# Half of each down projection by Strassen's scheme, in a float32 encoder block on one core

## The chip, the core and the metric

The kernel runs on one core of a Trainium2 chip. TensorE (PE in the profile; its weight loads are PEld) multiplies, VectorE (DVE) and ScalarE (ACT) work element by element, GpSimd (POOL) does next to nothing here, and SyncE (SP) issues the DMAs. The metric is the device time of one execution in microseconds. Less is better.

## The reference

One layer on x of 256 positions by 2048 channels, all in float32. Only the last part matters here:

```python
u = _rmsnorm(h, norm_mlp_g[layer])
a = jnp.einsum('bsd,df->bsf', u, w_up[layer])
a = jnp.square(jax.nn.relu(a))
h = h + jnp.einsum('bsf,fd->bsd', a, w_down[layer])
...
return _rmsnorm(h, norm_final_g)
```

w_up is 2048 x 8192, w_down 8192 x 2048. Before it come an input projection, a Fourier branch, eight heads of attention and an output projection; the change leaves their code alone.

## The kernel before

**Numbers.** A float32 operand is written as a high part, rounded for the fast matmul, and a low part, the rest. `split` (line 128) casts the high part on ScalarE and subtracts on VectorE. A product is three matmuls, high by high, high by low, low by high: `mm3` (line 138).

**Weights.** `_order` (line 39) lists the chunks of all weights, each a tile of 128 x 2048 (1 MB), in the order in which the program uses them. `load_next` (line 151) loads a chunk into `w_raw` and splits it into `w_hi` and `w_lo` in two halves of 1024 columns. `chunk` (line 179) hands out the next one and calls `load_next` so that AHEAD = 2 further chunks are under way. The pool has AHEAD + 1 = 3 buffers of each name, so a chunk is cast into the buffers of the chunk three earlier, once TensorE is through with that one.

**The MLP.** The 8192 hidden channels go in NGRP = 4 groups of 2048. In each group:

- 16 columns of the up projection (`column`, line 229): 16 matmuls of 128x512 with the high weights, then 16 of 128x256 with the low ones. `total` (line 260) adds the two halves of the result, `up` (line 558) applies relu, the norm's factor and the square, and splits the result into row j of `y_hi` and `y_lo`.
- 4 strips of the down projection (`strip`, line 204): each makes 512 output channels from four chunks, 24 matmuls of 128x512 per chunk (2 blocks of 128 positions by 4 rows by 3). The result is added to h (`gh` in the profile).

In the last group the fourth strip is the tail (from line 591). Its chunks are multiplied by `products`: the first 128 positions in one PSUM tile of 512 columns, the others in two of 256. The finished strips before it are squared, summed and multiplied by the final norm's weights on the way, and `ending` does the last norm and stores.

**Order.** Each engine runs its instructions in the order in which a scheduler has put them when the program is built. It may put later work ahead of an instruction that it expects to wait. The chunk loads keep the order of `_order` on SP's queue. PSUM has two pools of four tiles: `acc` for columns and strips, `aux` for the rest.

Of the kernel before, what the change touches and what calls it, by code (L numbers as in the profile page):

```python
# [29 lines left out]
CK = KT // NN  # L30
NGRP = DFF // D
AHEAD = 2
FIRST = (4, 4, 2, 2, 2)
WARM = 9
FEW = 224
MIDDLE = 11


def _order():

    todo = []

    def rows(name, row0, col0):
        todo.extend((name, row0 + c * CK * P, CK, col0, NS) for c in range(NN))

    def cols(name, col0):
        todo.append((name, 0, KT, col0, P))  # L50

    rows("w_in", 0, 0)
    rows("w_in", 0, NS)
    for a in range(2):
        rows("w_in", 0, 3 * FOURIER + a * NS)
        for hd in range(a * 4, a * 4 + 4):
            cols("w_in", FOURIER + hd * HD)
            cols("w_in", 2 * FOURIER + hd * HD)
    for n in range(NN):
        rows("w_out", 0, n * NS)  # L60
    for gi in range(NGRP):
        for j in range(KT):
            cols("w_up", gi * D + j * P)
        for n in range(NN):
            rows("w_down", gi * D, n * NS)
    return todo


# [1 line left out]
def tile_block(ctx: ExitStack, tc: tile.TileContext, gx_t, x, w_all, w_f, g_fin,  # L70
# [6 lines left out]
    ps_acc = ctx.enter_context(tc.tile_pool(name="ps_acc", bufs=4, space=bass.MemoryType.PSUM))  # L77
    ps_aux = ctx.enter_context(tc.tile_pool(name="ps_aux", bufs=4, space=bass.MemoryType.PSUM))

    def acc():  # L80
        return ps_acc.tile([P, NS], F32, name="acc")

    def aux():
        return ps_aux.tile([P, NS], F32, name="aux")
# [66 lines left out]
    def load_next():  # L151
        i = len(loaded)
        raw = wpool.tile([P, D], F32, name="w_raw")
        hi = wpool.tile([P, D], F32R, name="w_hi")
        lo = wpool.tile([P, D], F32R, name="w_lo")
        cuts = FIRST[i] if i < len(FIRST) else 1
# [12 lines left out]
        loaded.append((hi.rearrange("p (k n) -> p k n", k=nk), lo.rearrange("p (k n) -> p k n", k=nk)))  # L169

    def load_x(k0, nk):
        cols = slice(NG + k0 * S if k0 else 0, NG + (k0 + nk) * S)
# [53 lines left out]
                part()  # L226
        return ps

    def column(r, parts=None, need=None):

        ps = acc()
        hi, lo = chunk()

        def large(kt):
            nc.tensor.matmul(ps, hi[:, kt, :], r[:, kt, :], start=kt == 0, stop=False)  # L237

        def few_columns(kt):
            nc.tensor.matmul(ps[:, S:], lo[:, kt, :], r[:, kt, :S], start=False, stop=kt == KT - 1)  # L240
# [42 lines left out]
    def across(inv, room):  # L283

        ps = aux()[:, :S]
        for m in range(NM):
            b = room()
            nc.vector.tensor_scalar_mul(out=b, in0=ones, scalar1=inv[:, m:m + 1])
            nc.tensor.transpose(ps[:, m * P:(m + 1) * P], b, ident)
        return ps  # L290
# [257 lines left out]
    att_ctx.close()  # L548

    mlp = ctx.enter_context(tc.tile_pool(name="mlp", bufs=1))  # L550
    junk = mlp.tile([P, NS], F32, name="junk")
# [6 lines left out]
    def up(ps, hidden, j):  # L558
        r = mlp.tile([P, S], F32, name="relu", bufs=2)
        nc.vector.scalar_tensor_tensor(out=r, in0=total(ps, mlp), scalar=0.0, in1=inv_u, op0=ALU.max, op1=ALU.mult)  # L560
        q = mlp.tile([P, S], F32, name="sq", bufs=2)
        nc.scalar.activation(q, r, AF.Square)  # L562
        split(hidden[0][:, j, :], hidden[1][:, j, :], q)

    ss3 = small(NM * NN, NN)
    for gi in range(NGRP):
        pool = acts if gi % 2 else mlp
        hidden = [pool.tile([P, KT, S], F32R, name=f"y_{s}") for s in ("hi", "lo")]
        for j in range(KT):
            if gi == 0 and j == 0:  # L570
                ps = column(u2, parts=(4, 6, 8), need=KT - CK)
                inv2 = inverse(sums(ss2, "n2"), "n2")
                nc.vector.tensor_copy(out=inv_u, in_=across(inv2, lambda: mlp.tile([P, S], F32, name="relu", bufs=2)[:, :P]))
            else:
                ps = column(u2)
            up(ps, hidden, j)
        for n in range(NN):
            final = gi == NGRP - 1
            if final and n == NN - 1:
                break  # L580
            ps = strip(*hidden)
            ns = slice(n * NS, (n + 1) * NS)
            for m in range(NM):
                hs = h[m][:, ns]
                nc.vector.tensor_add(out=hs, in0=hs, in1=ps[m])  # L585
                if final:
                    squares(ss3, m, n)
                    nc.vector.tensor_mul(out=hs, in0=hs, in1=g_b[:, ns])


    NH2 = NS // 2
    tail = [[(acc(), slice(0, NS))], [(aux()[:, :NH2], slice(0, NH2)), (aux()[:, :NH2], slice(NH2, NS))]]
    base = small(NM)
    got = []

# [79 lines left out]
def _tiles(weights):  # L675

    todo = _order()
    out = np.empty((len(todo), P, D), np.float32)
    for i, (name, row0, nk, col0, n) in enumerate(todo):
        block = weights[name][row0:row0 + nk * P, col0:col0 + n]  # L680
        out[i] = block.reshape(nk, P, n).transpose(1, 0, 2).reshape(P, D)
    return out
# [27 lines left out]
```

## Time and profile before

| what | us |
|---|---|
| median of 3 runs | 1023.94 (1023.74 to 1024.06) |
| the profiled execution's own time | 1024.08 |
| its span, first to last instruction | 1022.3 |
| TensorE busy with matmuls | 1012.7 |
| VectorE busy | 610.7 |
| ScalarE busy | 496.3 |

The profile is of one execution. A row of a stretch (a window) gives its length, then for PE, PEld, DVE, ACT and POOL the busy us and, as (x..), the instructions, then the granted clock of TensorE (1.00 is full), the DMA engines' share and GB/s. A row of the timeline gives start, duration, engine, line, operation, output <- input, shape and count, and in brackets the idle time of the engine before it with what ended it. The busy time of matmuls is modelled, and they are pipelined: their spacing says more than their duration.

### The profile page before, as it was taken

What the parts mean: (1) busy time and instruction counts of PE and PEld (TensorE: products, weight loads), DVE (VectorE), ACT (ScalarE), POOL (GpSimd) and SP (SyncE); (2) the same over time, 40 slices, a digit from 0 to 9 for tenths busy, and PEclk for the clock granted to TensorE, in tenths of its full rate; (3) what the DMA queues carried; (4) which work ended last, traced back from release to release, by engine and by line L of the source; (5) the groups of instructions that cost most, each with busy time, mean ns of one, the idle gap of its engine ahead of it and who ended that gap; (6) DMA issues with size and microseconds to landing.
All of it is one profiled execution on the core that took longest, in us unless ns stands there. A gap on an engine that the chain in (4) does not pass through costs nothing.

```text
span 1022.3 us, 13002 instructions
## 1 busy us (share of the span) xinstructions
PE 1012.7 (99%) x5254; PEld 869.2 (85%) x5254; DVE 610.7 (60%) x846; ACT 496.3 (49%) x741; POOL 1.3 (0%) x10
## 2 busy tenths in 40 slices
PE   9999999999999999999999999999999999999997
PEld 7888888888888888888888888888888888888886
DVE  7975775775456665545656545556655446565553
ACT  7754645554446454333555433354543334554441
POOL 0000000000000000000000000000000000000000
PEclk9999999999999999999999999999999999999999
DMA  9663745444565554555555555555545555545532
GB/s 328 229 226 117 267 168 201 164 166 165 188 224 191 180 205 168 203 196 181 200 201 174 202 180 191 206 192 179 206 169 202 199 180 198 199 176 201 182 147 83
DMA packets 32683, 195.10 MB, mean 191 GB/s; under 512 B 3568, under 2 KB 6128, under 8 KB 10608
## 3 DMA queue, kind: packets, MB, share of 16 engines
q1 hardware_dynamic: 32624, 194.28, 53.7%
q8 instruction: 41, 0.67, 0.3%
q14 instruction: 18, 0.15, 0.0%
HBM read 192.17 MB, written 2.10 MB: 190 GB/s over the span
## 4 chain that ended last, share of the span: by engine, by line
PE 97%; DMA 1%; SPq 0%; DVE 0%; ACT 0%; issue 0%; ACTq 0%
PE acc L237 29%; PE acc L140 16%; PE acc L141 16%; PE acc L139 16%; PE acc L240 15%; PE aux L139 1%; PE aux L141 1%; PE aux L140 1%; DMA w_raw<-w_all 1%; SPq L93 0%; PE aux L538 0%; PE aux L493 0%; DVE w_lo L132 0%; ACT w_hi L131 0%; ACT gh L633 0%
## 5 line engine op out<-in xcount | busy, mean ns | idle before, releaser
L132 DVE TENSOR_TENSOR w_lo<-w_raw,w_hi 128x1024 fp32r<-128x1024 f32 (+1 forms) x356 | 424.0, 1209 | 281.0 <-ACT w_hi L131 204.0
L131 ACT CAST w_hi<-w_raw 128x1024 fp32r<-128x1024 f32 (+1 forms) x356 | 354.1, 1038 | 251.5 <-PE acc L141 228.2
L237 PE MATMUL acc<-u,w_hi 128*128 128x512 f32 x1280 | 309.5, 391 | 0.0
L237 PEld LDWEIGHTS acc<-u,w_hi 128*128 128x128 f32 x1280 | 234.8, 188 | 45.1
L139 PE MATMUL acc<-w_hi,y_hi 128*128 128x512 f32 x624 | 243.7, 391 | 0.0
L141 PE MATMUL acc<-w_hi,y_lo 128*128 128x512 f32 x624 | 242.9, 389 | 0.0
L140 PE MATMUL acc<-w_lo,y_hi 128*128 128x512 f32 x624 | 242.9, 389 | 0.0
L240 PEld LDWEIGHTS acc<-u,w_lo 128*128 128x128 f32 x1280 | 165.1, 191 | 6.2
L240 PE MATMUL acc<-u,w_lo 128*128 128x256 f32 x1280 | 168.4, 283 | 0.0
L141 PEld LDWEIGHTS acc<-w_hi,y_lo 128*128 128x128 f32 x624 | 117.2, 188 | 24.6
L140 PEld LDWEIGHTS acc<-w_lo,y_hi 128*128 128x128 f32 x624 | 117.2, 188 | 23.8
L139 PEld LDWEIGHTS acc<-w_hi,y_hi 128*128 128x128 f32 x624 | 117.2, 188 | 23.7
L562 ACT ACTIVATE sq<-relu 128x256 f32<-128x256 f32 x64 | 26.7, 418 | 160.7 <-DVE relu L560 160.7
L132 DVE TENSOR_TENSOR y_lo<-sq,y_hi 128x256 fp32r<-128x256 f32 x64 | 27.3, 426 | 58.8 <-ACT y_hi L131 58.8
L140 PE MATMUL acc<-w_lo,u 128*128 128x512 f32 x120 | 47.1, 392 | 0.5 <-DVE w_lo L132 0.5
L141 PE MATMUL acc<-w_hi,u 128*128 128x512 f32 x120 | 46.8, 390 | 0.0
L139 PE MATMUL acc<-w_hi,u 128*128 128x512 f32 x120 | 46.4, 393 | 0.3 <-ACT w_hi L131 0.3
L263 DVE TENSOR_TENSOR total<-acc,total 128x256 f32<-128x256 f32 x80 | 33.5, 418 | 2.7 <-ACT total L262 2.7
L262 ACT COPY total<-acc 128x256 f32<-128x256 f32 x80 | 29.2, 365 | 8.0 <-PE acc L240 8.0
L585 DVE TENSOR_TENSOR gh<-gh,acc 128x512 f32<-128x512 f32 x30 | 20.5, 684 | 16.8 <-PE acc L141 16.8
L140 PEld LDWEIGHTS acc<-w_lo,u 128*128 128x128 f32 x120 | 22.6, 188 | 5.2 <-DVE w_lo L132 1.1
L131 ACT CAST y_hi<-sq 128x256 fp32r<-128x256 f32 x64 | 26.0, 406 | 2.0
(141 smaller groups left out, 473.5 us busy)
## 6 DMA issues: line engine op xcount, KB each, us to landing
w_raw<-w_all SPq DMA_DIRECT2D x171, 1024.0 KB, 4.8
w_raw<-w_all SPq DMA_DIRECT2D x6, 512.0 KB, 7.9
w_raw<-w_all SPq DMA_DIRECT2D x8, 256.0 KB, 4.5
gh<-x SPq DMA_DIRECT2D x8, 256.0 KB, 7.1
out<-gh SPq DMA_DIRECT2D x6, 256.0 KB, 2.4
gh<-gx_t SPq DMA_DIRECT2D x4, 256.0 KB, 6.6
wf<-w_f SPq DMA_DIRECT2D x4, 256.0 KB, 4.9
g_b<-g_fin SPq DMA_DIRECT2D x1, 1024.0 KB, 4.3
```

The source lines that it names most:

```text
L131: nc.scalar.copy(out=hi, in_=src)
L132: nc.vector.tensor_tensor(out=lo, in0=src, in1=f32(hi), op=ALU.subtract)
L139: nc.tensor.matmul(ps, l_hi, r_hi, start=first, stop=False)
L140: nc.tensor.matmul(ps, l_hi, r_lo, start=False, stop=False)
L141: nc.tensor.matmul(ps, l_lo, r_hi, start=False, stop=last)
L237: nc.tensor.matmul(ps, hi[:, kt, :], r[:, kt, :], start=kt == 0, stop=False)
L240: nc.tensor.matmul(ps[:, S:], lo[:, kt, :], r[:, kt, :S], start=False, stop=kt == KT - 1)
L262: nc.scalar.copy(out=t, in_=ps[1])
L263: nc.vector.tensor_tensor(out=t, in0=ps[0], in1=t, op=ALU.add)
L562: nc.scalar.activation(q, r, AF.Square)
L585: nc.vector.tensor_add(out=hs, in0=hs, in1=ps[m])
```

## The change

In each group half of the down projection's work, output channels 0 to 1023, is done by Strassen's scheme in Winograd's form. The hidden activations are taken as 2 x 2 blocks: positions 0 to 127 and 128 to 255, hidden rows 0 to 7 and 8 to 15. The weights are also 2 x 2 blocks: the same rows by output channels 0 to 511 and 512 to 1023. The eight block products become seven. For this each of four blocks of activations and of four blocks of weights is a sum or difference of original ones, formed before the split into high and low parts. Output channels 1024 to 2047 are done as before ("plain").

- **`_mlp`** lists a group's steps. The columns now go in pairs, j and j + 8, and four of the eight *seven steps* lie between them; the other four lie between the chunks of the two plain strips. Step s takes one chunk that holds rows s and s + 8 of the weights for 1024 output channels, and makes six of the seven products, three matmuls each: 18 of 128x512 into six PSUM tiles, held from step 0 to step 7. The seventh product goes in two chunks of its own ("apart"), 12 matmuls each. In the last group the seven steps are packed closer towards the end, and the apart chunks go between them.
- **`quadrants`** prepares a seven step's chunk. VectorE makes four subtractions of 512 columns in place in `w_raw`, between these ScalarE casts two blocks into `b_hi`, and VectorE subtracts for `b_lo`; then `w_hi` and `w_lo` get the inner and the outer halves. So a chunk has three casts and seven VectorE instructions for two and two. `b_hi` and `b_lo` have one buffer each.
- **`sums_of`** makes the four sums of activations for a pair of columns: four VectorE instructions of 128 columns in place in `sq`, then a split of 512 columns into `s_hi` and `s_lo` (five buffers).
- **The sums of products.** In each group four of the products are added to `kept` (copied in the first), two straight into h, and the apart product into h. After the last group nine additions put `kept` into the four output blocks, and `weigh` squares and multiplies these. All of this lies in program order ahead of the tail's first chunk.
- **PSUM.** `acc` becomes two names of two tiles. The columns, plain strips and the apart product take `first`; two of the six products take `second`, four take `aux`. All groups now write the one `y_hi`, `y_lo`.

The core of the diff (the host's `_tiles` lays the 1 MB chunk out to match):

```diff
+    for j in range(HALF):
+        todo.extend((("up", j, 0), ("up", j + HALF, 0)))
+        if j in (2, 4, 6):
+            seven(j // 2 - 1)
+    seven(3)
...
+        p_hi = mlp.tile([P, 2, NS], F32R, name="b_hi")
+        p_lo = mlp.tile([P, 2, NS], F32R, name="b_lo")
...
+        nc.scalar.copy(out=p_hi, in_=pure)
+        less(b12, b12, b11)
+        less(p_lo, pure, f32(p_hi))
+        less(b22, b22, b12)
+        nc.scalar.copy(out=hi[:, inner], in_=raw[:, inner])
+        less(b11, b22, b11)
+        less(b21, b22, b21)
+        nc.scalar.copy(out=outer(hi), in_=outer(raw))
+        less(lo[:, inner], raw[:, inner], f32(hi[:, inner]))
+        less(outer(lo), outer(raw), f32(outer(hi)))
...
+                for ps, l, r in ((p1, tile_of(i, 0), b11), (p3, s4, b22), (p5, s1, t1), (p7, s3, t3),
+                                 (p6, s2, t2), (p4, tile_of(i + HALF, 1), t4)):
+                    mm3(ps, *l, *r, i == 0, i == HALF - 1)
+                if i == HALF - 1:
+                    for k, ps in ((k1, p1), (k5, p5), (k7, p7), (k6, p6)):
+                        if gi:
+                            add(k, ps)
+                        else:
+                            nc.scalar.copy(out=k, in_=ps)
+                    add(c12, p3)
+                    add(c21, p4, ALU.subtract)
...
+    add(c11, k1)
+    add(k6, k1)
+    for block, ks in ((c12, (k6, k5)), (c21, (k6, k7)), (c22, (k6, k5, k7))):
+        for k in ks:
+            add(block, k)
+    for m in range(NM):
+        for n in range(2):
+            weigh(m, n)
```

How it moves instructions is shown at three places. In these rows a number behind a name tells buffers apart, w_lo<-w_raw is the low half of a chunk's split, and line 189 is `split`, 244 a subtraction of `quadrants`, 353 and 650 a column's total and relu, 662 to 665 `sums_of`.

VectorE in the columns of the last group, before: one column after the other, five instructions each.

```order
L132 TENSOR_TENSOR w_lo_7386<-w_raw_7384,w_hi_7385 128x1024
L263 TENSOR_TENSOR total_7375<-acc_7333,total_7375 128x256
L132 TENSOR_TENSOR w_lo_7386<-w_raw_7384,w_hi_7385 128x1024
L560 SCALAR_TENSOR_TENSOR relu_7374<-total_7375,inv_k_2752 128x256
L132 TENSOR_TENSOR y_lo_6782<-sq_7379,y_hi_6781 128x256
```

The same engine and place now, around the chunk of seven step 2 (w_raw_7846):

```order
L244 TENSOR_TENSOR w_raw_7846<-w_raw_7846 128x512
L189 TENSOR_TENSOR w_lo_7791<-w_raw_7789,w_hi_7790 128x1024 x2
L353 TENSOR_TENSOR total_7781<-acc_7738,total_7781 128x256
L244 TENSOR_TENSOR b_lo_7851<-w_raw_7846,b_hi_7850 128x1024
L650 SCALAR_TENSOR_TENSOR relu_7780<-total_7781,inv_k_2751 128x256
L244 TENSOR_TENSOR w_raw_7846<-w_raw_7846 128x512 x2
L189 TENSOR_TENSOR y_lo_91<-sq_7779,y_hi_90 128x256
L244 TENSOR_TENSOR w_raw_7846<-w_raw_7846 128x512
L353 TENSOR_TENSOR total_7830<-acc_7788,total_7830 128x256
L244 TENSOR_TENSOR w_lo_7848<-w_raw_7846,w_hi_7847 128x1024
L650 SCALAR_TENSOR_TENSOR relu_7829<-total_7830,inv_k_2751 128x256
L244 TENSOR_TENSOR w_lo_7848<-w_raw_7846,w_hi_7847 128x2x512
```

The seven instructions of `quadrants` are spread between the instructions of two columns, so each engine's queue now holds three chains that take turns.

VectorE ahead of the tail's third and fourth chunk, before (w_lo_7998 and w_lo_8042; the additions to gh are the strip ahead):

```order
L132 TENSOR_TENSOR w_lo_7955<-w_raw_7953,w_hi_7954 128x1024 x2
L585 TENSOR_TENSOR gh_94<-gh_94,acc_7855 128x512
L588 TENSOR_TENSOR gh_94<-gh_94,g_b_2750 128x512
L585 TENSOR_TENSOR gh_94<-gh_94,acc_7856 128x512
L132 TENSOR_TENSOR w_lo_7998<-w_raw_7996,w_hi_7997 128x1024
L588 TENSOR_TENSOR gh_94<-gh_94,g_b_2750 128x512
```

The same place now, from the second tail chunk (w_lo_8429) to the third (w_lo_8472):

```order
L189 TENSOR_TENSOR w_lo_8429<-w_raw_8427,w_hi_8428 128x1024 x2
L682 TENSOR_TENSOR gh_94<-gh_94,acc_8374 128x512
L682 TENSOR_TENSOR kept_2752<-kept_2752 128x512
L682 TENSOR_TENSOR gh_94<-gh_94,kept_2752 128x512 x6
L687 TENSOR_TENSOR gh_94<-gh_94,g_b_2749 128x512
L682 TENSOR_TENSOR gh_94<-gh_94,kept_2752 128x512
L687 TENSOR_TENSOR gh_94<-gh_94,g_b_2749 128x512
L682 TENSOR_TENSOR gh_94<-gh_94,kept_2752 128x512
L687 TENSOR_TENSOR gh_94<-gh_94,g_b_2749 128x512
L189 TENSOR_TENSOR w_lo_8472<-w_raw_8470,w_hi_8471 128x1024
```

Thirteen instructions now stand between the two chunks' low halves, where three stood.

TensorE at the change from the second to the third tail chunk, before: straight on in the tile of the first 128 positions.

```order
L140 MATMUL acc_7991<-w_lo_7955,y_hi_6781 128x512
L141 MATMUL acc_7991<-w_hi_7954,y_lo_6782 128x512
L139 MATMUL acc_7991<-w_hi_7997,y_hi_6781 128x512
L140 MATMUL acc_7991<-w_lo_7998,y_hi_6781 128x512
L141 MATMUL acc_7991<-w_hi_7997,y_lo_6782 128x512
```

The same place now: after one matmul with the third chunk's high half (w_hi_8471) come 26 small ones, nearly all with the second chunk, of which the last four stand here, and then the first that reads w_lo_8472.

```order
L196 MATMUL aux_8467<-w_hi_8428,y_hi_90 128x256
L197 MATMUL aux_8467<-w_lo_8429,y_hi_90 128x256
L198 MATMUL aux_8467<-w_hi_8428,y_lo_91 128x256
L196 MATMUL aux_8467<-w_hi_8471,y_hi_90 128x256
L197 MATMUL acc_8465<-w_lo_8472,y_hi_90 128x512
L198 MATMUL acc_8465<-w_hi_8471,y_lo_91 128x512
```

The scheduler has drawn these products of the other 128 positions forward, ahead of the wait for VectorE.

More of the change, by code (lines that the diff above doesn't have):

```diff
@@ L36, with _mlp, seven, plain @@
 MIDDLE = 11
+def _mlp(gi):
+    todo = []
+    def seven(s):
+        todo.append(("seven", s, 0))
+    def plain(n, *cs):
+        todo.extend(("plain", n, c) for c in cs)
+    for j in range(HALF):
[3 more added lines that the diff above has]
+    seven(3)
+    if gi < NGRP - 1:
+        plain(2, 0, 1)
+        seven(4)
+        plain(2, 2, 3)
+        seven(5)
+        plain(3, 0, 1)
+        seven(6)
+        plain(3, 2, 3)
+        seven(7)
+        todo.extend((("apart", 0, 0), ("apart", 0, 1)))
+    else:
+        plain(2, 0)
+        seven(4)
+        plain(2, 1, 2)
+        seven(5)
+        plain(2, 3)
+        seven(6)
+        todo.append(("apart", 0, 0))
+        seven(7)
+        todo.append(("apart", 0, 1))
+        plain(3, 0, 1, 2, 3)
+    return todo
 def _order():
@@ L61, in _order @@
     for gi in range(NGRP):
[L62 to L65, printed above, removed]
+        for what, i, c in _mlp(gi):
+            if what == "up":
+                cols("w_up", gi * D + i * P)
+            elif what == "seven":
+                todo.append(("w_down", gi * D + i * P, 0, 0, NS))
+            elif what == "plain":
+                todo.append(("w_down", gi * D + c * CK * P, CK, i * NS, NS))
+            else:
+                todo.append(("w_down", gi * D + (HALF + c * CK) * P, CK, 0, NS))
     return todo
@@ L76, in tile_block, with first, second @@
     acts = ctx.enter_context(tc.tile_pool(name="acts", bufs=1))
[L77 removed]
+    ps_acc = ctx.enter_context(tc.tile_pool(name="ps_acc", bufs=2, space=bass.MemoryType.PSUM))
     ps_aux = ctx.enter_context(tc.tile_pool(name="ps_aux", bufs=4, space=bass.MemoryType.PSUM))
+    turn = [0]
     def acc():
+        turn[0] ^= 1
+        return first() if turn[0] else second()
+    def first():
         return ps_acc.tile([P, NS], F32, name="acc")
+    def second():
+        return ps_acc.tile([P, NS], F32, name="acc_2")
     def aux():
@@ L155, in load_next @@
         lo = wpool.tile([P, D], F32R, name="w_lo")
+        if not order[i][2]:
+            load(raw, w_all[i])
+            loaded.append(quadrants(raw, hi, lo))
+            return
         cuts = FIRST[i] if i < len(FIRST) else 1
@@ L227, in strip, with column @@
         return ps
-    def column(r, parts=None, need=None):
-        ps = acc()
+    def column(r, parts=None, need=None, room=acc):
+        ps = room()
         hi, lo = chunk()
@@ L556, in tile_block, with up @@
     inv_u = acts.tile([P, S], F32, name="inv_k")
-    def up(ps, hidden, j):
+    hidden = y_hi, y_lo
+    def up(ps, j, q):
         r = mlp.tile([P, S], F32, name="relu", bufs=2)
         nc.vector.scalar_tensor_tensor(out=r, in0=total(ps, mlp), scalar=0.0, in1=inv_u, op0=ALU.max, op1=ALU.mult)
-        q = mlp.tile([P, S], F32, name="sq", bufs=2)
         nc.scalar.activation(q, r, AF.Square)
         split(hidden[0][:, j, :], hidden[1][:, j, :], q)
-    ss3 = small(NM * NN, NN)
-    for gi in range(NGRP):
[L567 to L573, printed above, removed]
-            else:
[L575 to L588, printed above, removed]
@@ new lines, in sums_of @@
+    def sums_of(q):
+        a11, a21, a12, a22 = (flat(q)[:, i * P:(i + 1) * P] for i in range(4))
+        nc.vector.tensor_tensor(out=a22, in0=a21, in1=a22, op=ALU.add)
+        nc.vector.tensor_tensor(out=a21, in0=a11, in1=a21, op=ALU.subtract)
+        nc.vector.tensor_tensor(out=a11, in0=a22, in1=a11, op=ALU.subtract)
+        nc.vector.tensor_tensor(out=a12, in0=a12, in1=a11, op=ALU.subtract)
+        hi = mlp.tile([P, 4 * P], F32R, name="s_hi", bufs=5)
+        lo = mlp.tile([P, 4 * P], F32R, name="s_lo", bufs=5)
+        split(hi, lo, flat(q))
+        s2, s3, s4, s1 = ((hi[:, i * P:(i + 1) * P], lo[:, i * P:(i + 1) * P]) for i in range(4))
+        return s1, s2, s3, s4
@@ new lines, in tile_of, with add, weigh @@
+    def tile_of(j, m):
+        ms = slice(m * P, (m + 1) * P)
+        return hidden[0][:, j, ms], hidden[1][:, j, ms]
+    ss3 = small(NM * NN, NN)
+    kept = mlp.tile([P, 4, NS], F32, name="kept")
+    k1, k5, k6, k7 = (kept[:, i, :] for i in range(4))
+    c11, c12, c21, c22 = (h[m][:, n * NS:(n + 1) * NS] for m in range(NM) for n in range(2))
+    def add(out, other, op=ALU.add):
+        nc.vector.tensor_tensor(out=out, in0=out, in1=other, op=op)
+    def weigh(m, n):
+        ns = slice(n * NS, (n + 1) * NS)
+        nc.scalar.activation(junk, h[m][:, ns], AF.Square, accum_out=ss3[:, m, n:n + 1])
+        nc.vector.tensor_mul(out=h[m][:, ns], in0=h[m][:, ns], in1=g_b[:, ns])
@@ L591, in tile_block @@
+    add(c11, k1)
[3 more added lines that the diff above has]
+            add(block, k)
+    for m in range(NM):
+        for n in range(2):
+            weigh(m, n)
     NH2 = NS // 2
-    tail = [[(acc(), slice(0, NS))], [(aux()[:, :NH2], slice(0, NH2)), (aux()[:, :NH2], slice(NH2, NS))]]
+    tail = [[(first(), slice(0, NS))], [(aux()[:, :NH2], slice(0, NH2)), (aux()[:, :NH2], slice(NH2, NS))]]
     base = small(NM)
```

62 lines of the change are left out of this document (61 added, 1 removed).

## The prediction

> **What bounds the kernel now.** I read the profile's first page, then the stretches of the MLP, then the order of time inside one column, inside one strip, and at the end.
>
> The page: busy time of TensorE, the granted clock by slice, and the chain that ended last.
>
> ```profile
> span 1022.3 us, 13002 instructions
> PE 1012.7 (99%) x5254; PEld 869.2 (85%) x5254; DVE 610.7 (60%) x846; ACT 496.3 (49%) x741; POOL 1.3 (0%) x10
> PEclk9999999999999999999999999999999999999999
> PE 97%; DMA 1%; SPq 0%; DVE 0%; ACT 0%; issue 0%; ACTq 0%
> ```
>
> TensorE bounds everything: 97% of the chain that ended last is matmuls, at the full granted clock. So a matmul less is its spacing less, if nothing else comes up to take TensorE's place. The spacing is read from a stretch inside a strip of the down projection (busy time with counts, clock, DMA) and, for a column of the up projection, from three rows of the timeline:
>
> ```profile
> 399.83:418.19 18.36, 18.36 (x82) 15.21 (x81) 9.16 (x11) 6.84 (x8) 0.00 (x0) 1.00 0.47 174
> 340.86 2.08 PE L240 MATMUL acc<-u,w_lo 128*128 128x256 f32 x16
> 342.78 3.82 PE L237 MATMUL acc<-u,w_hi 128*128 128x512 f32 x16
> 346.43 2.08 PE L240 MATMUL acc<-u,w_lo 128*128 128x256 f32 x16
> ```
>
> The stretch begins and ends at a matmul's start: 82 matmuls are 81 spacings, 18.36/81 = 0.2267 us for one of 128x512. A column takes 346.43 - 340.86 = 5.57 us, a small matmul (342.78 - 340.86)/16 = 0.12 us. A strip's chunk of 24 matmuls takes 5.44 us.
>
> What VectorE has free beside that decides this change. One column's work on it, and on ScalarE:
>
> ```profile
> 343.03 1.23 DVE L132 TENSOR_TENSOR w_lo<-w_raw,w_hi 128x1024 fp32r<-128x1024 f32 x1 [1.19 <-PE acc L240]
> 344.18 0.42 DVE L263 TENSOR_TENSOR total<-acc,total 128x256 f32<-128x256 f32 x1
> 344.51 1.22 DVE L132 TENSOR_TENSOR w_lo<-w_raw,w_hi 128x1024 fp32r<-128x1024 f32 x1
> 345.64 0.42 DVE L560 SCALAR_TENSOR_TENSOR relu<-total,inv_k 128x256 f32<-128x256 f32 x1
> 346.98 0.42 DVE L132 TENSOR_TENSOR y_lo<-sq,y_hi 128x256 fp32r<-128x256 f32 x1 [0.92 <-ACT y_hi L131]
> 346.86 1.99 ACT L131 CAST w_hi<-w_raw 128x1024 fp32r<-128x1024 f32 x2
> ```
>
> Starts follow one another before the row ahead has ended, so two prices stand beside each other: the printed duration, and the spacing in a full queue. For 256 columns 0.42 and 344.51 - 344.18 = 0.33; for 1024 columns 1.22 and 345.64 - 344.51 = 1.13. For 512 and 128 columns there are rows elsewhere:
>
> ```profile
> 948.14 0.69 DVE L588 TENSOR_TENSOR gh<-gh,g_b 128x512 f32<-128x512 f32 x1 [0.79 <-ACT junk L519]
> 948.75 0.68 DVE L585 TENSOR_TENSOR gh<-gh,acc 128x512 f32<-128x512 f32 x1
> ...
> 316.20 0.48 DVE L288 TENSOR_SCALAR relu<-ones,few 128x128 f32<-128x128 f32 x2
> 316.60 1.22 DVE L132 TENSOR_TENSOR w_lo<-w_raw,w_hi 128x1024 fp32r<-128x1024 f32 x1
> ```
>
> 512 columns: 0.685 printed, 948.75 - 948.14 = 0.61 spaced. 128 columns: 0.2 spaced (two in 0.40), and about 0.28 printed, since the two overlap by 0.08 of their 0.48.
>
> **The change, part by part.**
>
> *TensorE.* A group's down projection had 4 strips of 4 chunks of 24, 384 matmuls of 128x512. Now it has 8 seven steps of 18 (144), 2 plain strips (192) and 2 apart chunks of 12 (24): 360. The columns keep theirs. Four groups save 4 x 24 = 96 matmuls of one shape and spacing: 96 x 0.2267 = **21.8 us**. A seven step takes 18 x 0.2267 = 4.08 us, an apart chunk 2.72.
>
> *VectorE's load.* A chunk to be split costs 2 x 1.13 = 2.3 us there. The seven step's chunk costs four subtractions of 512 and three low halves of 1024: 4 x 0.61 + 3 x 1.13 = 5.8 us (6.4 printed). A pair of columns adds four of 128 and one of 512: 4 x 0.2 + 0.61 = 1.4 us (1.8). Two columns and a seven step, the densest stretch of the column stage, are 11.14 + 4.08 = 15.2 us of TensorE; VectorE has 2 x (2.3 + 3 x 0.33) + 1.4 + 5.8 = 13.8 us spaced, or 2 x (2.44 + 1.26) + 1.8 + 6.4 = 15.6 printed. Two plain chunks and a seven step are 15.0 us against 2 x 2.3 + 5.8 = 10.4. I take the spaced price, since it is what a full queue shows; that such a load lets TensorE go on shows in two stretches of before, the second the attention stage, where VectorE's work comes in chains too:
>
> ```profile
> 20.00:30.00 10.00, 10.00 (x46) 8.28 (x45) 9.72 (x17) 9.39 (x14) 0.00 (x0) 1.00 0.84 312
> 100.00:200.00 100.00, 100.00 (x573) 87.85 (x572) 72.75 (x114) 54.46 (x95) 0.00 (x0) 1.00 0.57 203
> ```
>
> 97% and 73% busy by printed durations, and TensorE's busy time has no gap.
>
> *What the chain of a seven step waits for.* The queue is in order, so I went through it with these spacings for the last seven step of the column stage, zero at the start of the column behind seven step 2 (its end frees the buffers that seven step 3's chunk is cast into). VectorE comes to that chunk's b_lo at about -0.7, has both block differences written by 3.0 (the four subtractions of sq stand between them), the inner low half at 4.5 and the outer at 5.9 (ScalarE's three casts of 1.0 each lie one step ahead). Seven step 3 starts on TensorE at 11.1. Five us are left: the AHEAD of two chunks covers it. The column's own total is taken at 8.0, and the two PSUM tiles called first are wanted again only at 15.2. In the plain part the same walk leaves 1.5 to 5 us. So up to there I cost the new vector work at **nothing**, covered by two chunks of TensorE's work.
>
> *DMA.* 34 chunks a group for 32, on the same queue, each issued when the chunk three earlier has been split; the strip's stretch above moved 174 GB/s at a DMA share of 0.47, and 34/32 of the bytes in 0.97 of the time leaves half of it free. Nothing. ScalarE gets three casts of 1.0 where a chunk has two, and one of 512 per pair, on an engine that the page has busy for 49% of the span: hidden too.
>
> *The first columns.* TensorE ran ten matmuls of the second column before the two transposes of the norm; now they come straight after the first column. The norm's chain is also earlier in both queues (squares and square root ahead of the last four casts of u), by about the 1.6 us of these casts. Between 0 and the ten matmuls' 2.3 us; I take 0.
>
> *The end.* Here the cover goes. Behind the last seven step VectorE has six additions out of PSUM, then thirteen instructions (ten additions, three multiplications), all ahead of the third tail chunk's low half. Zero is the start of seven step 6 on TensorE. Its first two products free b_hi at 1.36; ScalarE's cast takes 1.05; from 2.5 VectorE is never idle: b_lo of step 7 1.13, two multiplications 1.2, three subtractions 1.9, its two low halves and an apart chunk's two 4.5, the first tail chunk 2.3, six additions 3.7, the second tail chunk 2.3, thirteen at 0.61 7.9, the third's first half 1.13: 26.0, so 28.5. TensorE gets there after 4.08 + 2.72 + 4.08 + 2.72, then 12 x 0.2267 + 24 x 0.12 = 5.6 and 2.72 for two tail chunks, then 0.23 and the 26 small products put ahead of the wait, 3.1: 25.3. It waits **3.2 us**, and another 0.6 for the second half (0.61 + 0.2 + 1.13 against six matmuls). By printed durations (24 of 512, 10 of 1024) the wait is 2.7 longer: the bounds are 0 and 6.5. I take 3.8, the value of the spacings. (Step 7's own low halves come with a few tenths to spare; TensorE's order there puts other products ahead of the late one.)
>
> The clock has to be watched in such a wait. The trace shows how long it stays up after the last matmul:
>
> ```profile
> 1014.36 0.28 PE L141 MATMUL aux<-w_hi,y_lo 128*128 128x256 f32 x1
> ...
> 1017.00:1018.00 1.00, 0.00 (x0) 0.00 (x0) 1.00 (x3) 1.00 (x2) 0.00 (x0) 1.00 0.09 32
> 1018.00:1019.00 1.00, 0.00 (x0) 0.00 (x0) 0.00 (x1) 0.07 (x1) 0.00 (x0) 0.86 0.82 278
> 1019.00:1020.00 1.00, 0.00 (x0) 0.00 (x0) 0.00 (x0) 0.00 (x0) 0.00 (x0) 0.50 1.04 387
> ```
>
> The last matmul ends at 1014.64; a mean of 0.86 between 1.00 and 0.50 puts the fall at 1018.7, 4.1 us later. My wait of 3.2 us stays under that. [...]
>
> **The sum.** Against the profiled execution, 1024.08 us, its span of 1022.3 and 1.8 around it: 1024.1 - 21.8 + 3.8 = **1006.1 us**. The median of the runs, 1023.94, is 0.1 lower; that is within what I can tell.
>
> **The rivals.**
>
> *The end is hidden after all.* If VectorE is some us ahead at seven step 6, or the wait falls where other products are ready, only the 21.8 go: 1024.1 - 21.8 = 1002.3. Against it: b_hi has one buffer, so VectorE can't start step 7's b_lo before TensorE is in step 6. Chance 0.12.
>
> *The clock falls in the wait at the end.* At printed durations TensorE idles 5.9 us, past the 4.1 of the trace. Behind the wait stand 23 matmuls of 0.2267 and 46 of 0.12, 10.7 us; at half clock for as long as it took to fall, 4.1 us, they lose 2: 1002.3 + 6.5 + 2 = 1011 (1019.5 if all of it runs at half). It turns on whether the idle passes about 4 us. [...] Chance 0.12.
>
> *A small wait per seven step in the columns.* Printed durations of 15.6 against 15.2 in the densest stretch: 0.4 us at each of 16 seven steps, 6.4 in all, 1006.1 + 6.4 = 1012.5. Chance 0.09.
>
> *Slower: VectorE becomes the bound of the column stage.* Printed durations, and the wait of 0.92 us for y_hi that every column shows now, no longer filled by other work since all of it hangs in one chain: 15.6 + 2 x 0.92 = 17.4 us against 15.2, 2.2 at each of 16 seven steps: 1006.1 + 35 = 1041. For it: the queue is in order and now mixes three chains that hand over to ScalarE. Against it: the 97% above. It decides from (1024.1 - 1006.1)/16 = 1.1 us at each of these steps on. Chance 0.06.
>
> That the change doesn't drop the matmuls is no rival: the instructions are counted.
>
> **How the numbers follow.** The forecast has 0.61, the rivals 0.12, 0.12, 0.09 and 0.06. The predicted time is the forecast's, 1006.1. The range goes from the hidden end, 1002, to 1013, which takes in the small waits and the mild fall of the clock. About 0.2% is what a measurement of this kernel can tell from no change, 2 us; only a state between the third and the last rival would fall in it. Faster 0.93, same 0.01, slower 0.06.
>
> **What would show it.** In the profile of the changed kernel TensorE has 96 matmuls of 128x512 fewer, spacing 0.227, and no gap above a few tenths before the last tail chunks; VectorE is at 80 to 95% in the column stage; before the third tail chunk TensorE waits about 3 us for w_lo, with the clock at 1.00. Wrong would be: waits of TensorE for VectorE at each seven step (the last two rivals), no gap at the end (the first), or a clock of 0.5 in the tail (the second).

## The result, and the profile after

| | us |
|---|---|
| before, beside it, median of 4 runs | 1023.86 |
| the changed kernel, median of 4 runs | 1006.53 (1005.87 to 1008.66) |
| ratio, 95% interval | 0.983 (0.982 to 0.985) |
| its profiled execution: time, span | 1005.87, 1004.1 |

The change makes the kernel 17.3 us faster; 1006.1 was predicted. The page of the changed kernel has the 96 matmuls fewer, and in the chain that ended last VectorE now has 4%:

```profile
span 1004.1 us, 13304 instructions
PE 991.3 (99%) x5158; PEld 850.4 (85%) x5158; DVE 797.1 (79%) x1199; ACT 565.8 (56%) x825; POOL 1.3 (0%) x10
PEclk9999999999999999999999999999999999999999
PE 93%; DVE 4%; DMA 1%; issue 1%; ACT 0%; SPq 0%; ACTq 0%
```

VectorE's load rose by 186 us, from 610.7 to 797.1. Whether any of it is paid is read from the stretches: the columns of the first group, its plain part, the last plain part, and the last 12 us before the third tail chunk.

```profile
314.00:412.00 98.00, 98.00 (x547) 85.88 (x546) 86.47 (x142) 63.50 (x98) 0.00 (x0) 1.00 0.64 227
412.00:490.00 78.00, 78.00 (x358) 65.09 (x358) 61.21 (x71) 41.34 (x47) 0.00 (x0) 1.00 0.64 224
920.00:973.00 53.00, 53.00 (x243) 43.87 (x243) 46.52 (x61) 28.96 (x36) 0.00 (x0) 1.00 0.54 204
973.00:985.00 12.00, 8.90 (x64) 8.17 (x62) 12.00 (x19) 7.32 (x13) 0.00 (x0) 1.00 0.24 99
```

In the first three TensorE is busy for the whole stretch, beside a VectorE that is busy for 88, 78 and 88% of it. In the fourth VectorE is busy without a gap and TensorE idles for 3.1 us. All waits of TensorE in the program (in total, times, longest):

```profile
PE acc L197 <- DVE w_lo L189: 3.6, 2, 3.1
PE aux L172 <- DVE ones L155: 1.1, 1, 1.1
PE acc L305 <- ACT w_hi L188: 0.2, 1, 0.2
```

The second and the third are the start of the program, and so is 0.5 of the first (at 17.87). What is left is one wait at the end. TensorE's timeline there:

```profile
981.58 0.28 PE L196 MATMUL aux<-w_hi,y_hi 128*128 128x256 f32 x1
984.96 0.50 PE L197 MATMUL acc<-w_lo,y_hi 128*128 128x512 f32 x1 [3.10 <-DVE w_lo L189]
```

The two starts are 3.38 apart where a small matmul takes 0.12: 3.26 us are lost. The wait for the second half loses another 0.3. VectorE's timeline gives the reason; of its rows these are b_lo of the last seven step, the second tail chunk, the thirteen instructions behind it with their first and their longest group, and the half that TensorE waits for:

```profile
958.91 1.23 DVE L244 TENSOR_TENSOR b_lo<-w_raw,b_hi 128x1024 fp32r<-128x1024 f32 x1
...
973.59 2.35 DVE L189 TENSOR_TENSOR w_lo<-w_raw,w_hi 128x1024 fp32r<-128x1024 f32 x2
975.87 0.68 DVE L682 TENSOR_TENSOR gh<-gh,acc 128x512 f32<-128x512 f32 x1
...
977.06 3.69 DVE L682 TENSOR_TENSOR gh<-gh,kept 128x512 f32<-128x512 f32 x6
...
983.69 1.22 DVE L189 TENSOR_TENSOR w_lo<-w_raw,w_hi 128x1024 fp32r<-128x1024 f32 x1
```

From 958.91 to 984.91, the end of the last row, are 26.0 us without a gap. Six instructions of 512 columns in 3.69 are five spacings and one printed duration: (3.69 - 0.685)/5 = 0.60 each.

### The profile page after: what moved, and what is told of

The parts are those of the page before. It is cut to its first block, busy times and chain, and to the rows that moved or that the text cites. A ratio compares the mean times of both kernels' runs of the same rounds, so it can differ in the third digit from the quotient of the medians.

```text
span 1004.1 us, 13304 instructions
## 1 busy us (share of the span) xinstructions
PE 991.3 (99%) x5158; PEld 850.4 (85%) x5158; DVE 797.1 (79%) x1199; ACT 565.8 (56%) x825; POOL 1.3 (0%) x10
## 4 chain that ended last, share of the span: by engine, by line
PE 93%; DVE 4%; DMA 1%; issue 1%; ACT 0%; SPq 0%; ACTq 0%
PE acc L327 29%; PE acc L330 15%; PE acc L197 12%; PE acc L198 12%; PE acc L196 12%; PE aux L197 4%; PE aux L196 4%; PE aux L198 4%; DVE w_lo L189 1%; DMA w_raw<-w_all 1%; DVE gh L682 1%; DVE w_lo L244 0%; SPq L150 0%; DVE gh L687 0%; DVE w_raw L244 0%
## 5 line engine op out<-in xcount | busy, mean ns | idle before, releaser
L189 DVE TENSOR_TENSOR w_lo<-w_raw,w_hi 128x1024 fp32r<-128x1024 f32 (+1 forms) x308 | 365.7, 1207 | 114.9 <-ACT w_hi L188 81.3
L188 ACT CAST w_hi<-w_raw 128x1024 fp32r<-128x1024 f32 (+1 forms) x308 | 309.4, 1037 | 184.9 <-PE acc L198 72.8
L197 PE MATMUL acc<-w_lo,y_hi 128*128 128x512 f32 x400 | 155.9, 390 | 3.2 <-DVE w_lo L189 3.1
L196 PE MATMUL acc<-w_hi,y_hi 128*128 128x512 f32 x400 | 156.5, 391 | 0.0
L198 PE MATMUL acc<-w_hi,y_lo 128*128 128x512 f32 x400 | 155.8, 389 | 0.0
L244 DVE TENSOR_TENSOR w_raw<-w_raw 128x512 f32<-128x512 f32 x128 | 86.4, 687 | 15.9 <-DMA w_raw<-w_all 14.6
L197 PEld LDWEIGHTS acc<-w_lo,y_hi 128*128 128x128 f32 x400 | 75.1, 188 | 19.0 <-DVE w_lo L189 3.9
L198 PEld LDWEIGHTS acc<-w_hi,y_lo 128*128 128x128 f32 x400 | 75.1, 188 | 15.8
L244 DVE TENSOR_TENSOR w_lo<-w_raw,w_hi 128x1024 fp32r<-128x1024 f32 x64 | 77.8, 1219 | 0.0
L250 ACT CAST w_hi<-w_raw 128x1024 fp32r<-128x1024 f32 x32 | 33.7, 1052 | 45.9 <-DVE w_raw L244 45.6
L253 ACT CAST w_hi<-w_raw 128x1024 fp32r<-128x1024 f32 x32 | 33.7, 1052 | 6.4 <-DVE w_raw L244 6.1
```

The lines of the kernel that those rows point to most:

```text
L188: nc.scalar.copy(out=hi, in_=src)
L189: nc.vector.tensor_tensor(out=lo, in0=src, in1=f32(hi), op=ALU.subtract)
L196: nc.tensor.matmul(ps, l_hi, r_hi, start=first, stop=False)
L197: nc.tensor.matmul(ps, l_hi, r_lo, start=False, stop=False)
L198: nc.tensor.matmul(ps, l_lo, r_hi, start=False, stop=last)
L244: nc.vector.tensor_tensor(out=out, in0=a, in1=b, op=ALU.subtract)
```

## The experiments

The theory is the prediction's: matmuls saved at their spacing; the vector work hidden in the columns and plain strips; one wait at the end, made by VectorE's in-order queue. Against it stood that the vector work costs a little everywhere, and that the wait has another cause. A second question came from the runs: four executions of one program between 1005.9 and 1008.7 us.

**The changed kernel again.** No edit; five runs.

> The changed kernel as it is, with more runs, so that the others have a partner on the same chip. Of its four runs so far two took 1005.9 and 1006.3 us at a mean granted clock of 0.998, two 1006.8 and 1008.7 at 0.995 and 0.994. Theory: the wait of 3.3 us at the end is close to the idle time after which the clock falls (4.1 us in the trace of before), so that the clock falls in some executions; then the runs split into about 1006 at 0.998 and 1007 to 1009 at 0.994 to 0.995. Rival: the spread has nothing to do with the clock; then the time does not go with the mean clock.

Measured: 1007.78 us (1006.98 to 1008.73), ratio 0.984 (0.983 to 0.985). Of the nine runs, four have a mean clock of 0.997 or 0.998 and 1005.9 to 1007.3 us, five 0.994 or 0.995 and 1006.8 to 1008.7. The profiled one (1008.73) shows why. Its waits at the end are the same, but the clock falls; stretches of one microsecond, then one of two that covers the fall after the last matmul:

```profile
983.26 0.28 PE L196 MATMUL aux<-w_hi,y_hi 128*128 128x256 f32 x1
986.61 0.50 PE L197 MATMUL acc<-w_lo,y_hi 128*128 128x512 f32 x1 [3.07 <-DVE w_lo L189]
```

```profile
986.00:987.00 1.00, 0.39 (x2) 0.35 (x3) 1.00 (x2) 0.00 (x0) 0.00 (x0) 1.00 0.00 0
987.00:988.00 1.00, 1.00 (x5) 0.84 (x4) 1.00 (x3) 0.00 (x0) 0.00 (x0) 0.80 0.00 0
988.00:989.00 1.00, 1.00 (x3) 0.50 (x3) 1.00 (x3) 0.00 (x0) 0.00 (x0) 0.50 0.00 0
...
991.00:992.00 1.00, 1.00 (x5) 0.79 (x5) 0.00 (x0) 0.00 (x0) 0.00 (x0) 0.99 0.00 0
...
1000.00:1002.00 2.00, 0.00 (x0) 0.00 (x0) 1.63 (x9) 0.82 (x2) 0.00 (x0) 0.81 0.32 121
```

A mean of 0.80 between 1.00 and 0.50 is a fall at 987.6, one microsecond after TensorE has gone on; it is back at 991.0, 3.4 us later. The last fall is at 1001.24, 10.2 us after that, three times 3.4; from the first fall to it are 13.64 us (13.64/4 = 3.41). In the first profile the clock is at 1.00 from 978 to 1000, and the fall after the last matmul is at 1000.68 (mean 0.92 from 999 to 1001). So the traces show a wait of 3.07 us with a fall and one of 3.10 without. An estimate from the distances in this trace: if the clock changes only at marks 3.41 us apart, the stretch from 984.2 to 987.6 holds 2.4 us of idle time here (up to 986.6), and marks counted back from 1000.68 would lie at 987.04 and 983.63 in the first profile and cut its wait into 1.8 and 1.3 us. That would tell the two executions apart; that it is the cause was not shown. The fall costs 1.2 us: from the end of the wait to the start of the last matmul are 12.41 us (986.61 to 999.02) against 11.20 (984.96 to 996.16). The two profiled executions differ by 2.86 at that matmul; the other 1.65 come from the start of the program, where the last wait ends at 19.52 in the one and at 17.87 in the other. So the spread has two sources, and only one of them is the change's. The other seven runs have no trace; the mean clock alone puts them in one group or the other.

The last matmul of the same profile stands ahead of the last fall:

```profile
999.02 0.28 PE L198 MATMUL aux<-w_hi,y_lo 128*128 128x256 f32 x1
```

It ends at 999.30, and the clock falls at 1001.24, 1.94 us later. In the first profile the last matmul ends at 996.44, and the clock falls 4.24 us later.

**The additions behind the tail's first products.** The final additions, the multiplications and the mean move down:

```diff
-    add(c11, k1)
-    add(k6, k1)
-    for block, ks in ((c12, (k6, k5)), (c21, (k6, k7)), (c22, (k6, k5, k7))):
...
-    mean(base, sums(ss3[:, :, :NN - 1], "n3"), EPS)
...
     for c in range(1, NN):
         got.append(chunk())
         products(0, 0, c)
+    add(c11, k1)
+    add(k6, k1)
+    for block, ks in ((c12, (k6, k5)), (c21, (k6, k7)), (c22, (k6, k5, k7))):
...
+    mean(base, sums(ss3[:, :, :NN - 1], "n3"), EPS)
     ending(0)
```

> The nine final additions, the four multiplications of weigh and the first three quarters of the final sum of squares stand behind the tail's products of the first 128 positions and ahead of ending, instead of ahead of the tail. Theory (TensorE's wait at the end is VectorE's queue, thirteen instructions ahead of the third tail chunk's low half): both waits go, 3.6 us less than the changed kernel, a span of 1000.5 and a time of 1002.3 us, and the runs no longer spread, since there is no idle time in which the clock could fall. Rival 1 (the chain from b_hi's one buffer sets it, not the additions): the wait stays at 3 us and so does the time. Rival 2 (the additions only come late somewhere else): the wait at w_lo goes, but ending starts later, and the time stays within 1 us of the changed kernel's.

Measured: 1003.77 us (1003.22 to 1003.94), ratio 0.980 (0.979 to 0.982), and 1003.10 when it ran once more (below). TensorE's waits, all of them at the start:

```profile
PE aux L172 <- DVE ones L155: 1.1, 1, 1.1
PE acc L196 <- ACT w_hi L188: 0.8, 1, 0.8
PE acc L197 <- DVE w_lo L189: 0.5, 1, 0.5
```

The wait at the end is gone and the runs lie within 0.7 us. So VectorE's queue is the cause, and b_hi's one buffer alone is not. (A second buffer for b_hi wasn't tried.) Counted from the last wait at the start to the start of the last matmul, late takes 974.49 us (18.74 to 993.23) and the changed kernel 978.29 (17.87 to 996.16): the end had cost 3.8. But the gain in the whole span, 1001.9 against 1004.1, is smaller than that. Part is the start, 0.9 (the last wait there ends at 18.74, not 17.87); and 0.7 come back at the end, as the second rival has it. The last matmul starts at 993.23 and the span ends 8.7 later, where it ends 7.9 later in the changed kernel (996.16 to 1004.1): VectorE is now busy without a gap into the last norm.

**A longer wait.** Four additions more ahead of the tail:

```diff
     add(c11, k1)
     add(k6, k1)
+    for _ in range(4):
+        nc.vector.tensor_tensor(out=k1, in0=k5, in1=k7, op=ALU.add)
```

> Four more vector additions of 512 columns (k1 = k5 + k7, where k1 is no longer needed) ahead of the third tail chunk's low half; the result stays the same. Both theories: the wait grows by 4 x 0.61 = 2.4 us, to an idle time of about 5.7 us. Theory (the clock falls after about 4 us without a matmul): the granted clock shows about 0.5 in the windows behind the wait in the profile, and the time is 2.4 + 2 to 4 us above the changed kernel's fast runs, 1010.5 to 1012.5. Rival (a wait of this size leaves the clock at 1.00, for instance because weight loads or small matmuls count): 2.4 us above, 1008.4, with the clock at 1.00.

Measured: 1011.41 us (1010.15 to 1012.71), ratio 0.988 (0.986 to 0.989). The wait is 6.1 long, 3.0 more for four instructions where I said 2.4: the scheduler also put the last of the four multiplications ahead, so it is five of 0.61. The clock falls, here for longer:

```profile
987.00:988.00 1.00, 0.00 (x0) 0.00 (x0) 1.00 (x3) 0.00 (x0) 0.00 (x0) 0.74 0.00 0
988.00:989.00 1.00, 0.58 (x1) 0.50 (x2) 1.00 (x3) 0.00 (x0) 0.00 (x0) 0.50 0.00 0
...
994.00:995.00 1.00, 1.00 (x5) 0.77 (x5) 0.00 (x0) 0.00 (x0) 0.00 (x0) 0.85 0.00 0
```

The fall is at 987.5, 5.2 us after the end of the last matmul ahead of the wait (982.27). From 987.5 to 994.3 are 6.8 us, twice 3.4: halfway, at 990.9, TensorE has been at work again for 2.5 us (since 988.42), and the clock stays at 0.50. The theory that the clock falls stands, the rival doesn't.

**No block sums.**

```diff
-        nc.scalar.copy(out=p_hi, in_=pure)
-        less(b12, b12, b11)
-        less(p_lo, pure, f32(p_hi))
...
+        for k in range(2):
+            ks = slice(k * D // 2, (k + 1) * D // 2)
+            split(hi[:, ks], lo[:, ks], raw[:, ks])
...
-                    sums_at[i - HALF] = sums_of(q)
+                    sums_at[i - HALF] = [tile_of(r, m) for r in (i - HALF, i) for m in range(NM)]
```

> Left out: the sums and differences of activations and of weights. A seven step's chunk is split like a plain one (two casts, two subtractions), and its 18 matmuls take the chunk's quarters and the hidden rows as they are; matmuls, loads and the additions out of PSUM are all there. Theory (the added vector and scalar work is hidden in the columns and the plain strips, and shows only in the chain to the last tail chunks): no change in the stages before 940 us, the wait at the end shrinks to between 0 and 0.6 us since the chain no longer begins at b_hi but at the end of the last seven step, 1002.3 to 1003 us. Rival (the vector work costs a few tenths at each seven step that the profile does not name): 1002 less 32 x 0.2 to 0.4, that is 990 to 996 us.

Measured: 1002.41 us (1001.76 to 1003.33), ratio 0.979 (0.978 to 0.980). From the last wait at the start to the start of the last matmul there are as many matmuls here as in the run late, and neither waits between. Without the sums:

```profile
17.70 0.50 PE L197 MATMUL acc<-w_lo,u 128*128 128x512 f32 x1 [0.50 <-DVE w_lo L189]
...
992.01 0.28 PE L198 MATMUL aux<-w_hi,y_lo 128*128 128x256 f32 x1
```

In the run late, with them:

```profile
18.74 0.50 PE L197 MATMUL acc<-w_lo,u 128*128 128x512 f32 x1 [0.52 <-DVE w_lo L189]
...
993.23 0.28 PE L198 MATMUL aux<-w_hi,y_lo 128*128 128x256 f32 x1
```

992.01 - 17.70 = 974.31 us against 993.23 - 18.74 = 974.49. The sums and differences of 32 seven steps, with their casts and low halves, cost 0.2 us where there is no wait at the end. The additions out of PSUM are in both runs.

**How much room is left.** The next three add vector subtractions at each seven step's chunk of the first three groups to late, which ran beside them once more:

```diff
+        made.append(0)
+        for _ in range(6 if len(made) <= 3 * HALF else 0):
+            nc.vector.tensor_tensor(out=spare, in0=b11[:, :384], in1=b12[:, :384], op=ALU.subtract)
```

> The kernel of the run late once more, as the partner on the same chip of the three that are built on it. It took 1003.2 to 1003.9 us there; the same is expected, with no fall of the clock ahead of the last matmul.

Measured: 1003.10 us (1002.79 to 1003.88), ratio 0.980 (0.978 to 0.981). As expected.

> late, with six more vector subtractions of 384 columns at each seven step's chunk of the first three groups (into a tile that nothing reads; the result stays the same). By an estimate between the prices of 256 and 512 columns one costs 0.47 us spaced and 0.55 printed, so 2.8 or 3.3 us at each of 24 chunks. Theory (what counts is the spacing in a full queue, and a stage's total): VectorE has 86.4 + 4 x 2.8 = 98 us of work in a group's column stage against 105.4 of TensorE, and 64 in the plain part against 65.3, so nothing shows: 1003.8 us, with small waits at most. Rival (printed durations count): 99.2 + 4 x 3.3 = 112 against 105.4 and 71 against 65.3, 12 us a group, 1041 us.

Measured: 1020.04 us (1018.70 to 1022.14), ratio 0.996 (0.995 to 0.998): between the two. Where it went is read from the start of seven steps on TensorE: the first and the fourth of the first group, the seventh, and the first of the second group. Late once more:

```profile
342.46 0.40 PE L196 MATMUL aux<-b_hi,y_hi 128*128 128x512 f32 x1
410.37 0.40 PE L196 MATMUL aux<-b_hi,y_hi 128*128 128x512 f32 x1
455.27 0.39 PE L196 MATMUL aux<-b_hi,y_hi 128*128 128x512 f32 x1
513.13 0.40 PE L196 MATMUL aux<-b_hi,y_hi 128*128 128x512 f32 x1
```

With six more subtractions:

```profile
342.72 0.40 PE L196 MATMUL aux<-b_hi,y_hi 128*128 128x512 f32 x1
410.62 0.40 PE L196 MATMUL aux<-b_hi,y_hi 128*128 128x512 f32 x1
456.73 0.39 PE L196 MATMUL aux<-b_hi,y_hi 128*128 128x512 f32 x1
518.84 0.40 PE L196 MATMUL aux<-b_hi,y_hi 128*128 128x512 f32 x1
```

In the traces one of the added subtractions costs 0.47 us when another instruction follows (one starts at 361.08, what is behind it at 361.55) and 0.59 when the next one writes the same tile. So six cost 3.1 us at a chunk where 2.8 were said, two 1.0 and ten 5.2. In the columns the stretch takes 67.91 and 67.90 us: 3.1 us more at each chunk, and nothing paid. By printed durations that stage would have been 7 us over.

From the last seven step of the columns to the next group's first it takes 102.76 and 108.22: 5.5 us more, of which 1.2 come before the seventh seven step and 4.3 behind its start. There the theory said nothing and fell. VectorE isn't full there, as a total would have it: it waits itself, for the load of the next seven step's chunk. The first and the last of these rows are the start of two such chunks, the second the last low half of the first:

```profile
450.87 1.16 DVE L250 TENSOR_TENSOR spare<-w_raw 128x384 f32<-128x384 f32 x2 [1.01 <-DMA w_raw<-w_all]
...
460.48 1.22 DVE L246 TENSOR_TENSOR w_lo<-w_raw,w_hi 128x1024 fp32r<-128x1024 f32 x1
...
466.45 1.16 DVE L250 TENSOR_TENSOR spare<-w_raw 128x384 f32<-128x384 f32 x2 [1.35 <-DMA w_raw<-w_all]
```

A chunk is loaded into the buffer of the chunk three earlier, once that is split, and in the plain part this is the seven step before. The split ends at 461.70, the load is there at 466.45, 4.75 us later: the loop takes 466.45 - 450.87 = 15.6 us, where TensorE needs 15.0 for a seven step and two plain chunks. So what bounds there is a loop of VectorE's work and a load through one buffer. The prediction's walk left 1.5 us as the least in that part (its working isn't shown), and the next run tests that.

> As more6, with two instead of six: 0.9 us spaced, 1.1 printed, more at each seven step's chunk of the first three groups. The walk along VectorE's queue in the prediction left 5 us in the columns and 1.5 us as the least in the plain part. more6, with 2.8 us, lost 0.0 in the columns and 5.3 us a group in the plain part and behind it. Theory (the walk's room): under 1.5 us, so nothing shows, late's 1003.1 to 1003.8. Rival (the plain part has no room at all, and every added us there is paid): 4 x 0.9 to 1.1 us in each of three groups, 11 to 13 us, 1014 to 1017.

Measured: 1003.46 us (1003.20 to 1003.64), ratio 0.980 (0.978 to 0.981). Nothing shows with 1.0 us more at a chunk, as the walk's room has it; the rival's 11 us aren't there.

> As more6, with ten instead of six. Theory (spacing): 86.4 + 4 x 4.7 = 105.2 us in the column stage against 105.4, nothing or little there, but in the plain part 71.3 against 65.3: TensorE waits for VectorE there, 6 us a group, 1022 us. Rival (printed durations): 121 against 105.4 and 79.5 against 65.3, 30 us a group, 1094 us.

Measured: 1081.78 us (1078.88 to 1084.07), ratio 1.057 (1.055 to 1.059). Neither figure is right. TensorE waits inside 18 seven steps, at the first product that takes the inner half in w_hi. Here they are in total, with number and longest, and one of them:

```profile
PE aux L196 <- ACT w_hi L255: 46.1, 18, 5.5
```

```profile
422.40 0.80 PE L196 MATMUL aux<-w_hi,s_hi 128*128 128x512 f32 x1 [4.21 <-ACT w_hi L255]
```

ScalarE's cast of that half waits in turn for VectorE's differences (89.6 us, 24 times). In the first group the waits begin in the columns: 0.95 us in the second seven step, 2.15 in the third, 4.21 in the fourth. So with 5.2 us more at each chunk VectorE falls behind there too, and what it is late by adds up from chunk to chunk.

The clock suffers: its mean is 0.980. Of the 76 us more than the span of late's second run, 1001.2, 46 are these waits. A mean clock of 0.980 against 0.998 is 0.018 x 1077/0.5 = 39 us at half clock. Matmuls of 128x512 are 0.43 us apart at half clock (starts at 989.00 and 989.43 in the run again) instead of 0.23, so this loses 18 us at most. The rest is not settled.

**The multiplications on GpSimd.** To late:

```diff
-        nc.vector.tensor_mul(out=h[m][:, ns], in0=h[m][:, ns], in1=g_b[:, ns])
+        (nc.gpsimd if n < 2 else nc.vector).tensor_mul(out=h[m][:, ns], in0=h[m][:, ns], in1=g_b[:, ns])
```

> late, with the four multiplications of weigh (512 columns each) on GpSimd in place of VectorE. In late the wait for w_lo is gone, but VectorE is busy without a gap from the last seven step on, and the time from the last matmul's end to the end of the span is 8.4 us where the changed kernel has 7.7. Theory (late's end is bound by VectorE): 4 x 0.61 = 2.4 us off that queue, the 0.7 us come back, 1003.0 us. Rival (GpSimd, whose price for this no run shows, holds up ending or slows VectorE's neighbours): the same as late or slower, 1003.8 to 1006.

Measured: 1005.33 us (1005.14 to 1008.14), ratio 0.982 (0.981 to 0.984): the rival. VectorE and GpSimd in the tail:

```profile
982.67 4.20 DVE L682 TENSOR_TENSOR gh<-gh,kept 128x512 f32<-128x512 f32 x5
...
991.32 1.17 DVE L756 TENSOR_SCALAR few<-few 128x2 f32<-128x2 f32 x1
```

```profile
982.92 1.59 POOL L687 TENSOR_TENSOR gh<-gh,g_b 128x512 f32<-128x512 f32 x1 [929.30 <-ACT sq L686]
986.57 3.17 POOL L687 TENSOR_TENSOR gh<-gh,g_b 128x512 f32<-128x512 f32 x2 [2.05 <-ACT sq L686]
991.17 1.29 POOL L687 TENSOR_TENSOR gh<-gh,g_b 128x512 f32<-128x512 f32 x1 [1.44 <-ACT sq L686]
```

And the same two of VectorE in late once more, with GpSimd idle:

```profile
982.50 3.10 DVE L682 TENSOR_TENSOR gh<-gh,kept 128x512 f32<-128x512 f32 x5
...
990.12 0.17 DVE L756 TENSOR_SCALAR few<-few 128x2 f32<-128x2 f32 x1
```

A multiplication takes 1.59 on GpSimd against 0.69 on VectorE, and what VectorE runs beside it takes longer: 1.1 us more for the five additions, 1.6 for the two behind them (2.89 where two take 1.29), and 1.0 for a tiny instruction on which the last norm hangs.

**Fewer additions.** To late: the nine final additions move into the last group's columns, and the last group's products go straight into the output blocks.

```diff
+                if final and i < HALF and i:
+                    for block, k in finals[2 * i - 2:2 * i]:
+                        add(block, k)
...
+                if i == HALF - 1 and final:
+                    add(c11, p1)
+                    add(c12, p3)
+                    add(c12, p5)
+                    add(c22, p5)
+                    add(c21, p7)
+                    add(c22, p7)
+                    nc.scalar.copy(out=k6, in_=p6)
+                    add(k6, p1)
+                    add(c21, p4, ALU.subtract)
...
+    for block in (c12, c21, c22):
+        add(block, k6)
```

> late, with the nine final additions made on the first three groups' sums, in the last group's columns, where VectorE has room; the last group's products go straight into the output blocks: nine instructions in place of six behind the last seven step and three in place of nine in the tail, so four of 0.61 us fewer on VectorE between the last seven step and ending. Theory (late's 0.7 us between the last matmul and the end too much is VectorE's queue, busy without a gap from the last seven step on): the 2.4 us cover it, 0.7 us below late, 1002.4 to 1003.0 us against 1003.1 to 1003.8, with 7.7 us from the last matmul's end to the end of the span. Rival (ending waits for something else, or the three more additions out of PSUM ahead of the tail's chunks hold up TensorE): as late, or up to 1.2 us slower.

Measured: 1003.47 us (1002.68 to 1005.16), ratio 0.980 (0.979 to 0.982). In the profile (the fastest of the five runs) the end is as the theory has it: the last matmul starts at 992.98 and the span ends 7.9 later, at 1000.9. But the median isn't below late's, and the runs scatter by 2.5 us; what the slower ones lose isn't in the one profile. So the 0.7 at the end is shown, and a gain in time is not. By their medians this kernel and late (1003.77 and 1003.10) can't be told apart; late's runs scatter less.

## Why the prediction was right

*TensorE.* 5254 - 5158 = 96 matmuls fewer, 21.8 us by their spacing. The span fell by 1022.3 - 1004.1 = 18.2, and 21.8 less the 3.57 of waits at the end is 18.2. That these meet so closely is in part luck, since the start of the profile after is 0.4 us quicker (17.87 against the 18.29 below). Without the start, the stretch from the last wait there to the start of the last matmul settles it:

```profile
18.29 0.50 PE L140 MATMUL acc<-w_lo,u 128*128 128x512 f32 x1 [0.53 <-DVE w_lo L132]
```

Before it is 1014.36 - 18.29 = 996.07 us, without the sums 974.31: 21.8 less. The changed kernel's 978.29 is 3.8 above late's 974.49, and 3.8 is the term of the sum.

*VectorE's load, and its chain.* Costed at nothing. The run without the sums has 0.2 us for all of it. The walk holds in the changed kernel: the last low half for the last seven step of the first group's columns ends at 405.57 in its trace, and the step starts at 410.20, so 4.6 us are left where the walk had 5.2. As a rule for added work it is too simple. 3.1 us more at each chunk are free in the columns, but 5.2 make TensorE wait 7.3 us in three steps, because lateness is carried over. In the plain part 1.0 is free and 3.1 are not (1.5 said at the least). Totals by stage, which I used for the later expectations, missed both: a stage's sum can fit while a loop through one buffer doesn't.

*Spaced or printed price.* Spaced. Printed durations would have given waits in the columns with six more subtractions; there were none. But the spacing depends on what follows: 0.59 against 0.47 us above.

*DMA and ScalarE.* In the changed kernel the waits name neither behind the start of the program. *The first columns.* Taken at 0, between 0 and 2.3: TensorE's idle time in the first 20 us was 1.95 us before and is 1.86, and 2.96 in the profile of the run again. Executions differ there by more than the change does.

```profile
0.00:20.00 20.00, 18.05 (x75) 14.41 (x76) 12.52 (x23) 14.75 (x27) 0.70 (x6) 1.00 0.89 313
```

```profile
0.00:20.00 20.00, 18.14 (x77) 14.18 (x78) 13.01 (x24) 15.31 (x27) 0.70 (x6) 1.00 0.90 312
```

*The end.* A chain of 26.0 from b_lo and a wait of 3.2 were predicted, 26.0 and 3.26 measured; 0.6 for the second half, measured 0.3; the first matmul behind each of the two waits takes 0.1 more, which makes up the 3.8. Moving the thirteen instructions takes both away. The four additions added by hand cost what they must.

*The clock: the step that failed.* "My wait of 3.2 us stays under that" took 4.1 us, the time from the last matmul to the fall in one profile, for a limit. It isn't one. A wait of 3.10 us was spared in one execution and one of 3.07 hit in another. After the last matmul, where TensorE stays idle, the fall came 4.1 us later in before and 1.94 in the run again. What decides was not shown; that it is where the wait lies between such marks is only the estimate above. So the rival "the clock falls" was not on the other side of a threshold from the forecast: both happen, in different executions of one program. Its price was about right (2 us said, 1.2 measured), and by the two groups of clocks the nine runs' means are 1006.6 and 1008.1. The forecast is that of the first group; more than half of the executions belong to the second. So the 0.4 us between the forecast and the median of the first four runs are in part luck: a fall costs little, and two of the four were spared.

*The rivals.* The hidden end is what late makes by hand, 1003.1 to 1003.8 against the 1002.3 said. Small waits per seven step and a VectorE that bounds the columns: no wait is there, and it takes between 1.0 and 3.1 us more per chunk before one comes in the plain part, and between 3.1 and 5.2 in the columns.

## What to carry to other kernels

Work added to an engine that is 60% busy cost 0.2 us here, where each chain of it fitted the lead of the loads, and 5.2 us more at each chunk made TensorE wait; walk the queue at the densest place, and once round each buffer from load to load, since a stage's totals hide where it doesn't fit. Look for what a scheduler leaves in the queue ahead of the last loads: there no later work covers it, and moving such work down a few lines was worth 3 to 4 us here. Don't plan an idle time of TensorE of 3 us as safe for its clock: one of 3.07 us was followed by a fall here, one of 3.10 was not.

## What the runs showed of the hardware

The clock: in the run again the fall and the rise are 3.4 us apart, the rise and the next fall 10.2; in the run longwait the fall and the rise are 6.8 apart. In the run again the fall came 1.0 us after the matmuls had gone on. From the end of the last matmul to the fall were 4.1 us in before, 4.24 in the changed kernel's first profile and 1.94 in the run again. A wait of 3.10 us passed at 1.00 in the changed kernel's first profile; one of 3.07 in the run again and one of 6.15 in the run longwait had a fall. How much idle time makes the clock fall was not shown.

VectorE beside GpSimd at work takes longer: five additions of 512 columns took 4.20 us beside a GpSimd multiplication of 1.59 and 3.10 without, two took 2.89 where two take 1.29, and a tiny instruction took 1.17 beside a multiplication of 1.29 and 0.17 without. Why was not shown.
